# Delta rule of the prompt in a two-layer hybrid decoder step: both chunks' scores and triangular inverses side by side

## The chip, the cores and the metric

The kernel runs on one core of one Trainium2 chip. The metric is device time in microseconds (us), the median of several executions. The kernel is one inference step of a two-layer decoder, 256 prompt tokens and 64 sample tokens (8 sequences of 8), with all weights read once from memory.

## The reference, cut to what matters

Each layer projects the 320 tokens with one big matrix, runs three mixers side by side (a gated delta rule, differential attention on a paged cache, gated linear attention), projects back, and runs a gated feed-forward network. What the change touches is the gated delta rule of the prompt. It works in chunks of tokens; inside a chunk it solves a unit lower triangular system for each head:

```python
kk = jnp.einsum('bihd,bjhd->bhij', ki, ki)
A = jnp.where(strict, kk * dmat * bh[..., :, None], 0.0)
M = jnp.eye(C, dtype=jnp.float32) + A
sol = lax.linalg.triangular_solve(M, jnp.concatenate([vbeta, kbd], -1), left_side=True, lower=True, unit_diagonal=True)
u = sol[..., :DV] - jnp.einsum('bhck,bhkv->bhcv', sol[..., DV:], S)
o = (q * exp(gh)) @ S + qk @ u ;  S_new = S * exp(glast) + kw^T @ u
```

There are 6 heads of 128 x 128. The kernel uses chunks of 128 tokens for the prompt, so two chunks (c = 0, 1), and treats the heads in two halves of three (hs = 0, 1). The scores and the inverse of M do not depend on the running state S; only what follows them does.

## The kernel before, in words

**The dense stream.** Weights come in units of 128 x 512 numbers (`raw`), are split into a high part (`whi`, ACT) and a low part (`wlo`, DVE), and multiplied on PE with the activations (`xh`, `xl`, and `oA`, `oB`, `act..` in the later projections), three matmuls of 128x320 for each 128 x 128 block. There are 19392 such dense matmuls in a program; their order is fixed. They are recorded by `emit_unit` (L1035); the rest of the work (the mixers, normalisation) is written as tasks (generators) that are stepped between units and record their operations too. The output projection's first unit needs `oA`, the gated result of the delta rule, and everything else that it reads (L1062 `drain`).

**What sets the order.** All operations are first recorded with their dependences, then `order` (L536) makes a list schedule: for each engine it takes the available operation with the longest tail. On PE it has three classes, dense matmuls, small matmuls that fill the array, and small matmuls on 32- or 64-row tiles ("part"), and it holds part work back until enough of it has gathered or one has waited long:

```python
sticky, PB, PW = False, 1000.0, 3000.0                      # L578
elif part and (0 not in cl or sum(ops[i].cost for i in part) >= PB or t - min(ops[i].est for i in part) >= PW):  # L610
    want = 2
```

Once issued, the order on each engine is that of the program: an instruction whose inputs are late holds up all that stand behind it on its engine. All instructions carry the line of the helper that issues them, L696 (DMA issues of the cache pages: L2031), so in the profile they are told apart by their tiles. `g` (in programs `g_0_90`, `g_1_...`) is the private memory of the delta rule of the prompt, `gen` and `geng` are the two general memories, `c` and `blkC` belong to the linear attention, `bank` is PSUM.

**The delta rule tasks.** `gdn_prompt(l, hs)` (L1647) treats one half: for each chunk it makes the decayed scores (`decay_scores`, L1602; `AQ` holds query and key scores), the inverses of the 32 x 32 diagonal blocks by five levels of masked products (`inverse`, L1553), assembles the 128 x 128 inverse in a block `U` of its own, and then applies it to values and state. The two halves use the same 2700 words (L1652), so the second starts when the first has ended; inside a half, chunk 1 started when chunk 0 had ended.

`gdn_sample(l, hs)` (L1795) is the same for the 64 sample tokens. It treats its three heads one after the other in one buffer: a head's state is loaded (`in_sgdn`, 512 KB, L1816), multiplied with keys and queries, updated, and stored (`out_gs`, L1863); only then can the next head's state be loaded. The second half (hs = 1) takes its 1920 and 704 words from the general memory `mem` (L1799), where the attention task holds 3640 words (L1920) until its last values are done (`attn_values`, L2121, released at L1947). The gated linear attention (`gla_main`, L2172) starts behind a flag that this sample task sets when it has its memory (L1802). When prompt and sample halves have ended, `gdn_main` (L1440) multiplies with the gate (`gate`, L1533) and writes `oA`, which the output projection waits for.

Of the kernel before, what the change touches and what calls it, by code (L numbers as in the profile page):

```python
# [18 lines left out]
ALU = mybir.AluOpType  # L19
# [724 lines left out]
def emit(nc, pool, psp, T, O, coff, ioff, n_pages):  # L744
# [63 lines left out]
    def cs(name, rows=slice(0, 128)):  # L808
        a, n = coff[name]
        return cst[rows, a:a + n]  # L810
# [91 lines left out]
    def ap(h):  # L902
        return h[1][2]
# [649 lines left out]
    def inverse(aq, k, R, get, keep):  # L1553

        nb = R // 32
        lv = (1, 2, 4, 8, 16) if R == 128 else (1, 2, 4)
        nl = len(lv)
        Ad = yield from get(32 * k)
        ad = ap(Ad)[0:R].rearrange("p (h i) -> p h i", h=k)
        for b in range(nb):  # L1560
            sl = slice(32 * b, 32 * b + 32)
            (G.tensor_copy if b % 2 else V.tensor_copy)(ad[sl], aq[sl, :, 1, sl])
        LT = yield from get(nl * 32 * k)
        lt = ap(LT)[0:R].rearrange("p (s h i) -> p s h i", s=nl, h=k)
        msk = cs("ms", slice(0, R)).rearrange("p (s i) -> p s i", s=5)[:, 0:nl]
        for s in range(nl):
            tt(V, lt[:, s], ad, msk[:, s:s + 1, :].to_broadcast([R, k, 32]), ALU.mult)
        fr(Ad)
        yield
        TU = yield from keep(64 * k)  # L1570
        tu = ap(TU)[0:R].rearrange("p (t h i) -> p t h i", t=2, h=k)
        idb = cs("idb", slice(0, R))[:, None, :].to_broadcast([R, k, 32])
        tf, tf_ = (ap(TU)[0:R, 32 * k * t:32 * k * t + 32 * k] for t in range(2))
        tt(V, tu[:, 1], idb, lt[:, 0], ALU.subtract)
        V.transpose(tf, tf_)
        yield
        Ph = yield from get(32 * k)
        p_ = ap(Ph)[0:R].rearrange("p (h i) -> p h i", h=k)
        for s in range(1, nl):
            bb = yield from bank()  # L1580
            pv_ = banks[bb][0:R, 0:32 * k].rearrange("p (h i) -> p h i", h=k)
            for h in range(k):
                for b in range(nb):
                    sl = slice(32 * b, 32 * b + 32)
                    mm(pv_[sl, h], lt[sl, s, h], tu[sl, 0, h])
            A.copy(p_, pv_)
            fb(bb)
            yield
            bb = yield from bank()
            pw = banks[bb][0:R, 0:32 * k].rearrange("p (h i) -> p h i", h=k)  # L1590
            for h in range(k):
                for b in range(nb):
                    sl = slice(32 * b, 32 * b + 32)
                    mm(pw[sl, h], tu[sl, 1, h], p_[sl, h])
            tt(V, tu[:, 0], tu[:, 0], pw, ALU.subtract)
            fb(bb)
            V.transpose(tf_, tf)
            yield
        fr(LT, Ph)
        return TU  # L1600

    def decay_scores(l, g, h0, k, get, keep):  # L1602

        X = L
        col = X["col"]
        c0, n = CC[g]
        R = n
        bb = yield from bank()
        b = banks[bb][0:R, 0:k * n].rearrange("p (h i) -> p h i", h=k)
        mng = cs("mneg") if g < 2 else cs("mneg8", slice(0, 64))  # L1610
        for h in range(k):
            tr(b[:, h], col["gc"][0:R, g, h0 + h:h0 + h + 1].to_broadcast([R, R]), slice(0, R))
        Dh = yield from get(k * n)
        d = ap(Dh)[0:R].rearrange("p (h i) -> p h i", h=k)
        for h in range(k):
            stt(d[:, h], b[:, h], col["gc"][0:R, g, h0 + h:h0 + h + 1], mng, ALU.subtract, ALU.add)
        fb(bb)
        A.activation(d, d, AF.Exp)
        yield
        AQ = yield from keep(k * 2 * n)  # L1620
        aq = ap(AQ)[0:R].rearrange("p (h t i) -> p h t i", h=k, t=2)
        for h in range(k):
            bb = yield from bank()
            b = banks[bb][0:R, 0:2 * n].rearrange("p (t i) -> p t i", t=2)
            for t, nm in enumerate(("q", "k")):
                mm(b[:, t], X["k"][:, h0 + h, c0:c0 + n], X[nm][:, h0 + h, c0:c0 + n])
            stt(aq[:, h], b, col["s"][0:R, g, h0 + h:h0 + h + 1], d[:, h:h + 1, :].to_broadcast([R, 2, n]), ALU.mult, ALU.mult)
            fb(bb)
            if h == 1:
                yield  # L1630
        yield
        fr(Dh)
        return AQ, aq

    def rms_factor(m, out, t1, c=None):

# [10 lines left out]
    def gdn_prompt(l, hs):  # L1647
# [3 lines left out]
        h0 = 3 * hs  # L1651
        R, M = yield from private(2700, lambda: (mem4[0],))  # L1652
        get = lambda n: get_from(n, lambda: (M,))
        for c in range(2):
            cc = slice(c * 128, c * 128 + 128)
            AQ, aq = yield from decay_scores(l, c, h0, 3, get, get)
            TU = yield from inverse(aq, 3, 128, get, get)
            tu = ap(TU).rearrange("p (t h i) -> p t h i", t=2, h=3)
            U = yield from get(384)
            u = ap(U).rearrange("p (h i) -> p h i", h=3)  # L1660
            G.memset(ap(U), 0.0)
            for b in range(4):
                sl = slice(32 * b, 32 * b + 32)
                (G.tensor_copy if b % 2 else A.copy)(u[sl, :, sl], tu[sl, 1])
            bb = yield from bank()
            pv_ = banks[bb][:, 0:96].rearrange("p (h i) -> p h i", h=3)
            for h in range(3):
                for a in range(2):
                    up, lo = slice(64 * a, 64 * a + 32), slice(64 * a + 32, 64 * a + 64)
                    mm(pv_[lo, h], aq[up, h, 1, lo], tu[up, 0, h])  # L1670
            Ph = yield from get(96)
            p_ = ap(Ph).rearrange("p (h i) -> p h i", h=3)
            for a in range(2):
                lo = slice(64 * a + 32, 64 * a + 64)
                A.copy(p_[lo], pv_[lo])
            fb(bb)
            T64 = yield from get(192)
            t64 = ap(T64).rearrange("p (h i) -> p h i", h=3)
            G.memset(ap(T64)[0:64], 0.0)
            V.tensor_copy(t64[0:32, :, 0:32], tu[0:32, 0])  # L1680
            V.tensor_copy(t64[32:64, :, 32:64], tu[32:64, 0])
            yield
            bb = yield from bank()
            pv_ = banks[bb][:, 0:96].rearrange("p (h i) -> p h i", h=3)
            for h in range(3):
                for a in range(2):
                    up, lo = slice(64 * a, 64 * a + 32), slice(64 * a + 32, 64 * a + 64)
                    mm(pv_[up, h], p_[lo, h], tu[lo, 1, h])
                mm(pv_[32:64, h], tu[32:64, 1, h], p_[32:64, h])
            for a in range(2):  # L1690
                up, lo = slice(64 * a, 64 * a + 32), slice(64 * a + 32, 64 * a + 64)
                tsc(V, u[up, :, lo], pv_[up], -1.0, ALU.mult)
            A.mul(t64[32:64, :, 0:32], pv_[32:64], -1.0)
            fb(bb)
            fr(TU, Ph)
            yield
            bb = yield from bank()
            pv_ = banks[bb][:, 0:192].rearrange("p (h i) -> p h i", h=3)
            for h in range(3):
                mm(pv_[64:128, h], aq[0:64, h, 1, 64:128], t64[0:64, h])  # L1700
            P64 = yield from get(192)
            p64 = ap(P64).rearrange("p (h i) -> p h i", h=3)
            A.copy(p64[64:128], pv_[64:128])
            fb(bb)

            bb = yield from bank(2)
            for h in range(3):
# [8 lines left out]
                A.mul(kw[:, h], banks[bb[0]][:, h * 128:h * 128 + 128], col["es"][:, c, h0 + h:h0 + h + 1])  # L1716
                tsc(V, vs[:, h], banks[bb[1]][:, h * 128:h * 128 + 128], col["nk"][:, c, h0 + h:h0 + h + 1], ALU.mult)
            fb(*bb)
            yield
            bb = yield from bank()  # L1720
            pv_ = banks[bb][:, 0:192].rearrange("p (h i) -> p h i", h=3)
            for h in range(3):
                mm(pv_[0:64, h], p64[64:128, h], u[64:128, h, 64:128])
            tsc(V, u[0:64, :, 64:128], pv_[0:64], -1.0, ALU.mult)
            fb(bb)
            fr(P64, T64)

            if c == 1:
                bb = yield from bank()
# [7 lines left out]
            bb = yield from bank()  # L1737
            b = banks[bb][:, 0:384].rearrange("p (h v) -> p h v", h=3)
            for h in range(3):
                mm(b[:, h], u[:, h], vs[:, h])  # L1740
            WS = yield from get(384)
            ws = ap(WS).rearrange("p (h v) -> p h v", h=3)
            A.copy(ws, b)
            fb(bb)
            fr(U, VS)
            OH = yield from get(384)
            o = ap(OH).rearrange("p (h v) -> p h v", h=3)
            if c == 1:
# [7 lines left out]
            bb = yield from bank()  # L1756
            b = banks[bb][:, 0:384].rearrange("p (h v) -> p h v", h=3)
            for h in range(3):
                mm(b[:, h], aq[:, h, 0], ws[:, h])
            if c == 1:  # L1760
                tt(V, o, o, b, ALU.add)
            else:
                V.tensor_copy(o, b)
            fb(bb)
            fr(AQ)
            bb = yield from bank()
            b = banks[bb][:, 0:384].rearrange("p (h v) -> p h v", h=3)
            for h in range(3):
# [26 lines left out]
    def gdn_sample(l, hs):  # L1795
# [5 lines left out]
        get = lambda n: get_from(n, lambda: (M1,))  # L1801
        set_flag(("gsmem", l, hs))  # L1802
        tmp = lambda n: get_from(n, lambda: (M2,))
        AQ, aq = yield from decay_scores(l, 2, h0, 3, tmp, get)
        TU = yield from inverse(aq, 3, 64, tmp, get)

        osm = ap(AQ)[64:128].rearrange("p (h v) -> p h v", h=3)
# [826 lines left out]
```

## Time and profile before

| | us |
|---|---|
| median of 3 runs | 3294.72 |
| lowest and highest of them | 3292.67 and 3296.1 |
| the profiled execution's own time | 3294.52 |
| its span (first to last instruction) | 3292.7 |
| PE busy | 3235.2 (98%) |
| PE weight loads busy | 3072.3 (93%) |
| DVE, ACT, POOL busy | 1959.6, 1493.2, 359.7 (60%, 45%, 11%) |
| mean granted TensorE clock | 0.994 of full speed |

PE busy is the union of modelled matmul durations; a matmul's duration (0.31 us for a dense one) is longer than the distance to the next one, so the pace of the dense stream is read by counting matmuls in a stretch. The delta rule of a layer lies in the first part of the layer (about 60 to 560 us in layer 0, 1700 to 2193 us in layer 1), between dense matmuls of the input projection.

### The profile page before, as it was taken

The page shows a single profiled execution, that of the slowest core. Times are in us where ns is not written, and L with a number is a line of the kernel's source. Part 1 is how long each engine was busy: PE and PEld are TensorE (multiplying, and loading weights), DVE is VectorE, ACT ScalarE, POOL GpSimd, SP SyncE. Part 2 cuts the span into 40 slices and gives each one's busy share as a digit, 9 for nine tenths or more (in the row PEclk, how much of TensorE's full clock was granted, in tenths as well). Part 3 has the DMA queues.
Part 4 walks back from the last instruction along what each step waited for, and adds up shares of the span by engine and source line. Part 5 has one row for each costly group of instructions (what it writes and reads, how often), then busy time and mean ns, then how long its engine had stood idle before and what let it go on. Part 6 is the DMA issues. An engine that isn't in the chain of part 4 may idle for free.

```text
span 3292.7 us, 67703 instructions
## 1 busy us (share of the span) xinstructions
PE 3235.2 (98%) x25466; PEld 3072.3 (93%) x25466; DVE 1959.6 (60%) x3780; ACT 1493.2 (45%) x3069; POOL 359.7 (11%) x604
## 2 busy tenths in 40 slices
PE   9999999999999999999999999989999999999997
PEld 9987887899999999999999887878999999999997
DVE  5676558885444445544776764588854544454446
ACT  5454444465433443344574444444744334433444
POOL 0233323200000000000002333231000000000000
PEclk9999999999999999999999999999999999999998
DMA  7466764455555555555555667534555555555553
GB/s 228 142 194 212 220 194 129 137 148 157 151 149 150 151 151 148 151 150 151 150 154 154 193 217 231 170 127 138 147 151 151 151 149 150 151 150 149 150 151 115
DMA packets 264393, 527.70 MB, mean 160 GB/s; under 512 B 31362, under 2 KB 33026, under 8 KB 263938
## 3 DMA queue, kind: packets, MB, share of 16 engines
q1 hardware_dynamic: 243586, 456.26, 48.4%
q0 software_dynamic: 20480, 67.13, 6.3%
q8 instruction: 199, 3.26, 0.4%
q14 instruction: 128, 1.05, 0.1%
HBM read 506.25 MB, written 16.36 MB: 159 GB/s over the span
## 4 chain that ended last, share of the span: by engine, by line
PE 76%; issue 2%; DVE 1%; DMA 1%; ACT 0%; POOL 0%; POOLq 0%; SPq 0%; ACTq 0%; DVEq 0%
PE bank L696 76%; DVE gen L696 0%; POOLq L2029 0%; DMA geng<-in_ck 0%; DVE wlo L696 0%; DVE geng L696 0%; POOL geng L2031 0%; DVE blkB L696 0%; DMA out_gs<-gen 0%; DMA gen<-in_sgdn 0%; DMA c<-in_sgdn 0%; ACT blkB L696 0%; DVE c L696 0%; POOL blkB L696 0%; ACT accq L696 0%
## 5 line engine op out<-in xcount | busy, mean ns | idle before, releaser
L696 DVE TENSOR_TENSOR wlo<-raw,whi 128x512 fp32r<-128x512 f32 x1616 | 1124.2, 696 | 1091.4 <-PE bank L696 893.5
L696 ACT CAST whi<-raw 128x512 fp32r<-128x512 f32 x1616 | 1001.7, 620 | 1403.6 <-PE bank L696 1340.0
L696 PE MATMUL bank<-xh,wlo 128*128 128x320 f32 (+1 forms) x4544 | 1418.6, 312 | 0.0
L696 PE MATMUL bank<-xh,whi 128*128 128x320 f32 (+1 forms) x4544 | 1413.3, 311 | 4.7 <-ACT xh L696 4.7
L696 PE MATMUL bank<-xl,whi 128*128 128x320 f32 (+1 forms) x4544 | 1414.6, 311 | 0.1
L696 PEld LDWEIGHTS bank<-xh,whi 128*128 128x128 f32 x4544 | 856.1, 188 | 12.8 <-issue 5.7
L696 PEld LDWEIGHTS bank<-xh,wlo 128*128 128x128 f32 x4544 | 857.8, 189 | 7.6 <-issue 3.9
L696 PEld LDWEIGHTS bank<-xl,whi 128*128 128x128 f32 x4544 | 855.4, 188 | 7.6 <-issue 4.4
L696 PE MATMUL bank<-actA,whi 128*128 128x320 f32 x1152 | 255.5, 309 | 0.0
L696 PEld LDWEIGHTS bank<-actA,whi 128*128 128x128 f32 x1152 | 192.9, 188 | 0.4
L696 PE MATMUL bank<-actA,wlo 128*128 128x320 f32 x576 | 178.1, 309 | 0.0
L696 PE MATMUL bank<-actB,whi 128*128 128x320 f32 x768 | 170.5, 309 | 0.0
L696 PE MATMUL bank<-actCh,whi 128*128 128x320 f32 x448 | 138.3, 309 | 0.0
L696 PE MATMUL bank<-actCl,whi 128*128 128x320 f32 x448 | 138.3, 309 | 0.0
L696 PE MATMUL bank<-actCh,wlo 128*128 128x320 f32 x448 | 138.3, 309 | 0.0
L696 PEld LDWEIGHTS bank<-actB,whi 128*128 128x128 f32 x768 | 128.6, 188 | 0.0
L696 PE MATMUL bank<-actB,wlo 128*128 128x320 f32 x384 | 118.6, 309 | 0.0
L696 PE MATMUL bank<-geng,gen 128*32 128x256 f32 (+5 forms) x968 | 101.8, 466 | 7.3 <-DMA geng<-in_ck 4.4
L696 PEld LDWEIGHTS bank<-actA,wlo 128*128 128x128 f32 x576 | 108.2, 188 | 0.1
L696 POOL COPY gen<-g 128x24 f32<-128x24 f32 x18 | 5.9, 328 | 878.1 <-DMA g<-in_scv 871.2
L2031 POOL DMA_DIRECT2D geng<-in_ck x128 | 70.7, 552 | 274.3 <-DVE actA L696 137.8
L696 PE MATMUL bank<-oA,whi 128*128 128x320 f32 x384 | 92.7, 325 | 5.3 <-ACT oA L696 4.8
(291 smaller groups left out, 3324.1 us busy)
## 6 DMA issues: line engine op xcount, KB each, us to landing
raw<-in_wgu SPq DMA_DIRECT2D x704, 256.0 KB
raw<-in_win SPq DMA_DIRECT2D x434, 256.0 KB
raw<-in_wd SPq DMA_DIRECT2D x352, 256.0 KB
geng<-in_ck POOLq DMA_DIRECT2D x128, 256.0 KB, 3.8
geng<-in_cvp POOLq DMA_DIRECT2D x128, 256.0 KB, 3.7
raw<-in_wout SPq DMA_DIRECT2D x128, 256.0 KB
c<-in_sgdn SPq DMA_DIRECT2D x6, 512.0 KB
out_gs<-c SPq DMA_DIRECT2D x6, 512.0 KB
```

What stands on the lines that cost most here:

```text
L696: fn(*[real(x) for x in a], **{k: real(v) for k, v in kw.items()})
L2031: G.eng.dma_start(out[:, k * 512:k * 512 + 512], src[l, ds(reg, 1)].rearrange(pat))
```

## The change

`inverse` no longer makes all masked copies of the diagonal blocks at once (`LT` of five parts) but one level at a time, in one buffer that is rewritten after each level's product. `gdn_prompt` makes the scores of both chunks first, into one `AQ` of 1536 words, then one inverse for six (chunk, head) pairs, and assembles it in place over the key scores (`u = aq[:, :, 1, :]`) instead of in a cleared block `U`. What follows (values, state, output) stays one chunk after the other, with the last product of the assembly moved ahead of it. `decay_scores` writes where its caller says. The sample task calls the same `inverse` and `decay_scores`.

```diff
@@ inverse
-        LT = yield from get(nl * 32 * k)
-        for s in range(nl):
-            tt(V, lt[:, s], ad, msk[:, s:s + 1, :].to_broadcast([R, k, 32]), ALU.mult)
-        fr(Ad)
+        LT = yield from get(32 * k)
+        def level(s):
+            tt(V, lt, ad, msk[:, s:s + 1, :].to_broadcast([R, k, 32]), ALU.mult)
+        level(0)
...
+        level(1)
...
-                    mm(pv_[sl, h], lt[sl, s, h], tu[sl, 0, h])
+                    mm(pv_[sl, h], lt[sl, h], tu[sl, 0, h])
             A.copy(p_, pv_)
             fb(bb)
+            if s + 1 < nl:
+                level(s + 1)
@@ gdn_prompt
+        AQ = yield from get(1536)
+        aq = ap(AQ).rearrange("p (h t i) -> p h t i", h=6, t=2)
+        u = aq[:, :, 1, :]
+        for c in range(2):
+            yield from decay_scores(l, c, h0, 3, get, aq[:, 3 * c:3 * c + 3])
+        TU = yield from inverse(aq, 6, 128, get, get)
...
+                mm(pv_[lo, h], u[up, h, lo], tu[up, 0, h])
...
         for c in range(2):
             cc = slice(c * 128, c * 128 + 128)
-            AQ, aq = yield from decay_scores(l, c, h0, 3, get, get)
-            TU = yield from inverse(aq, 3, 128, get, get)
...
-            U = yield from get(384)
-            G.memset(ap(U), 0.0)
...
-                mm(b[:, h], u[:, h], vs[:, h])
+                mm(b[:, h], u[:, 3 * c + h], vs[:, h])
...
-            fr(AQ)
+            M.release((AQ[1][0] + 768 * c, 768, None))
```

The list schedule is made anew, so the change moves instructions on every engine. Three places on PE, in layer 0.

First, a level of the inverse (`g` is the private memory of the prompt's delta rule), between dense matmuls of the input projection. Before:

```order
L696 MATMUL bank_80<-xl,whi 128x320
L696 MATMUL bank_80<-xh,wlo 128x320
L696 MATMUL bank_86<-cst,gen 128x128 x2
L696 MATMUL bank_85<-g_0_90 32x32 x12
L696 MATMUL bank_80<-xh,whi 128x320
```

Now:

```order
L696 MATMUL bank_81<-xl,whi 128x320
L696 MATMUL bank_81<-xh,wlo 128x320
L696 MATMUL bank_83<-g_0_90 32x32 x24
L696 MATMUL bank_81<-xh,whi 128x320
L696 MATMUL bank_81<-xl,whi 128x320
```

Two groups of 12 products on 32 x 32 tiles have become one of 24.

Second, the sample task's last head: the product of its state with keys and queries (`bank<-gen,sq` and `bank<-gen,sk`), with what stands ahead of it. Before:

```order
L696 MATMUL bank_80<-xl,whi 128x320
L696 MATMUL bank_80<-xh,wlo 128x320
L696 MATMUL bank_80<-xh,whi 128x320
L696 MATMUL bank_84<-gen,sq_625 32x512
L696 MATMUL bank_84<-gen,sk_91 32x512
L696 MATMUL bank_84<-gen,sq_625 32x512
L696 MATMUL bank_84<-gen,sk_91 32x512
L696 MATMUL bank_83<-geng 32x32 x12
L696 MATMUL bank_82<-geng 32x32 x4
```

Now:

```order
L696 MATMUL bank_85<-cst,sk_91 64x128
L696 MATMUL bank_85<-cst,sv 64x128
L696 MATMUL bank_81<-xh,wlo 128x320
L696 MATMUL bank_82<-gen,sq_625 32x512
L696 MATMUL bank_82<-gen,sk_91 32x512
L696 MATMUL bank_82<-gen,sq_625 32x512
L696 MATMUL bank_82<-gen,sk_91 32x512
L696 MATMUL bank_83<-geng 32x32 x12
L696 MATMUL bank_86<-geng 32x32 x4
```

The dense matmul just ahead of it is number 2509 of the program before; now it is number 2592, the last one of the input projection.

Third, what stands directly ahead of the output projection's first matmul on `oA`. Before:

```order
L696 MATMUL bank_81<-xh,whi 128x320
L696 MATMUL bank_81<-xl,whi 128x320
L696 MATMUL bank_81<-xh,wlo 128x320
L696 MATMUL bank_83<-cst,gen 64x128 x3
L696 MATMUL bank_79<-oA_6182,whi 128x320 x2
```

Now:

```order
L696 MATMUL bank_84<-gen 32x128 x2
L696 MATMUL bank_86<-geng 32x32 x4
L696 MATMUL bank_85<-geng 32x32 x4
L696 MATMUL bank_82<-geng 32x32 x4
L696 MATMUL bank_83<-gen 64x128
L696 MATMUL bank_82<-gen 128x512
L696 MATMUL bank_85<-gen 128x512
L696 MATMUL bank_84<-geng 32x32 x6
L696 MATMUL bank_86<-geng 32x32 x6
L696 MATMUL bank_83<-geng 32x32 x6
L696 MATMUL bank_84<-cst,gen 128x64 x3
L696 MATMUL bank_86<-geng 32x32 x6
```

Behind the last row follows the same first matmul on `oA`. The sample task's steps for its last head (`gen`) and some of the linear attention (`geng`) stand there where dense matmuls of the input projection stood before.

## Rows read from the trace of the kernel before

**Rows 1.** Section 1 of the page: busy time, share, instructions of each engine.

```profile
PE 3235.2 (98%) x25466; PEld 3072.3 (93%) x25466; DVE 1959.6 (60%) x3780; ACT 1493.2 (45%) x3069; POOL 359.7 (11%) x604
```

**Rows 2.** Busy time by stretch: stretch and length, engines' busy time (x instructions), clock.

```profile
1200.00:1500.00 300.00, 300.00 (x2048) 299.84 (x2048) 144.95 (x234) 117.31 (x199) 0.00 (x0) 1.00 0.55 150
```

**Rows 3.** PE's timeline (start, duration) round one group of the inverse.

```profile
276.88 0.31 PE L696 MATMUL bank<-xl,whi 128*128 128x320 f32 x1
277.12 0.39 PE L696 MATMUL bank<-g 32*32 32x32 f32 x24
277.44 0.41 PE L696 MATMUL bank<-xh,wlo 128*128 128x320 f32 x1
```

**Rows 4.** All PE products on `g`: durations min/median/max in ns, starts, forms.

```profile
L696 PE MATMUL bank<-g x2016: 188/191/276, 127.2 to 2091.2; 32*32 32x32 f32 x162, 128*128 128x128 f32 x13, 64*64 64x64 f32 x9
```

**Rows 5.** PE's timeline: two attention steps, and the second sample half's first product.

```profile
443.86 1.06 PE L696 MATMUL bank<-geng,gen 128*32 128x512 f32 x8
...
450.70 1.06 PE L696 MATMUL bank<-geng,gen 128*32 128x512 f32 x8
...
471.97 0.33 PE L696 MATMUL bank<-sq,sk 128*64 128x64 f32 x2
```

**Rows 6.** Timeline of PE and SP: the first head's state load of that half.

```profile
493.01 0.25 PE L696 MATMUL bank<-gen 32*32 32x32 f32 x4
...
493.36 0.33 SPq L696 DMA_DIRECT2D gen<-in_sgdn  x1
...
497.60 0.59 PE L696 MATMUL bank<-gen,sq 128*32 128x512 f32 x1
```

**Rows 7.** Timeline of PE and SP: from the second head's update to the third's product.

```profile
527.97 1.13 PE L696 MATMUL bank<-gen 32*128 32x512 f32 x4
...
534.96 0.33 SPq L696 DMA_DIRECT2D gen<-in_sgdn  x1
...
538.64 0.59 PE L696 MATMUL bank<-gen,sq 128*32 128x512 f32 x1 [1.51 <-DMA gen<-in_sgdn]
```

**Rows 8.** Timeline of all engines: from the third head's product to `oA`.

```profile
541.69 0.97 DVE L696 SCALAR_TENSOR_TENSOR gen<-gen 64x128 f32<-64x128 f32 x1
...
544.85 0.41 PE L696 MATMUL bank<-gen 32*32 32x128 f32 x4
...
546.63 0.38 PE L696 MATMUL bank<-geng 64*32 64x32 f32 x12 [1.37 <-DVE geng L696]
...
548.45 0.43 PE L696 MATMUL bank<-gen 64*64 64x128 f32 x2
...
555.73 0.37 PE L696 MATMUL bank<-cst,gen 64*128 64x64 f32 x3 [1.24 <-DVE gen L696]
...
558.26 2.85 POOL L696 TENSOR_TENSOR blkB<-blkB,sv 128x320 f32<-128x320 f32 x1 [3.09 <-ACT whi L696]
...
561.23 0.86 POOL L696 TENSOR_TENSOR blkB<-blkB,sv 128x320 f32<-128x320 f32 x1
...
562.63 0.41 PE L696 MATMUL bank<-oA,whi 128*128 128x320 f32 x1 [2.48 <-ACT oA L696]
```

**Rows 9.** Dense matmuls on `whi` (two of three) in that stretch, by stretch.

```profile
538.60:562.60 24.00, 12.95 (x55) 1.00 0.33 101
```

**Rows 10.** Dense matmuls on `wlo` (one of three) in that stretch.

```profile
538.60:562.60 24.00, 8.66 (x28) 1.00 0.33 101
```

**Rows 11.** PE's timeline, layer 1: the same two ends.

```profile
2169.39 0.59 PE L696 MATMUL bank<-gen,sq 128*32 128x512 f32 x1 [1.84 <-DMA gen<-in_sgdn]
...
2193.25 0.41 PE L696 MATMUL bank<-oA,whi 128*128 128x320 f32 x1 [2.31 <-ACT oA L696]
```

**Rows 12.** PE's timeline behind the first products on `oA`: a linear attention step.

```profile
579.83 0.75 PE L696 MATMUL bank<-cst,blkC 128*128 128x128 f32 x3 [1.67 <-DVE gen L696]
```

**Rows 13.** Busy time by stretch: a stretch of 3.4 us at a low granted clock.

```profile
580.00:583.40 3.40, 3.40 (x16) 3.40 (x16) 1.24 (x3) 0.28 (x3) 0.00 (x0) 0.50 0.22 82
```

More of the change, by code (lines that the diff above doesn't have):

```diff
@@ L1562, in inverse @@
             (G.tensor_copy if b % 2 else V.tensor_copy)(ad[sl], aq[sl, :, 1, sl])
-        LT = yield from get(nl * 32 * k)
-        lt = ap(LT)[0:R].rearrange("p (s h i) -> p s h i", s=nl, h=k)
-        msk = cs("ms", slice(0, R)).rearrange("p (s i) -> p s i", s=5)[:, 0:nl]
-        for s in range(nl):
-            tt(V, lt[:, s], ad, msk[:, s:s + 1, :].to_broadcast([R, k, 32]), ALU.mult)
-        fr(Ad)
+        LT = yield from get(32 * k)
+        lt = ap(LT)[0:R].rearrange("p (h i) -> p h i", h=k)
+        msk = cs("ms", slice(0, R)).rearrange("p (s i) -> p s i", s=5)
+        def level(s):
+            tt(V, lt, ad, msk[:, s:s + 1, :].to_broadcast([R, k, 32]), ALU.mult)
+        level(0)
         yield
@@ L1573, in inverse @@
         tf, tf_ = (ap(TU)[0:R, 32 * k * t:32 * k * t + 32 * k] for t in range(2))
-        tt(V, tu[:, 1], idb, lt[:, 0], ALU.subtract)
+        tt(V, tu[:, 1], idb, lt, ALU.subtract)
         V.transpose(tf, tf_)
+        level(1)
         yield
@@ L1598, in inverse, with decay_scores @@
             yield
-        fr(LT, Ph)
+        fr(Ad, LT, Ph)
         return TU
-    def decay_scores(l, g, h0, k, get, keep):
+    def decay_scores(l, g, h0, k, get, aq):
         X = L
@@ L1619, in decay_scores @@
         yield
-        AQ = yield from keep(k * 2 * n)
-        aq = ap(AQ)[0:R].rearrange("p (h t i) -> p h t i", h=k, t=2)
         for h in range(k):
@@ L1632, in decay_scores @@
         fr(Dh)
-        return AQ, aq
     def rms_factor(m, out, t1, c=None):
@@ L1653, in gdn_prompt @@
         get = lambda n: get_from(n, lambda: (M,))
+        AQ = yield from get(1536)
[4 more added lines that the diff above has]
+        TU = yield from inverse(aq, 6, 128, get, get)
+        tu = ap(TU).rearrange("p (t h i) -> p t h i", t=2, h=6)
+        bb = yield from bank()
+        pv_ = banks[bb][:, 0:192].rearrange("p (h i) -> p h i", h=6)
@@ new lines, in gdn_prompt @@
+        for h in range(6):
+            for a in range(2):
+                up, lo = slice(64 * a, 64 * a + 32), slice(64 * a + 32, 64 * a + 64)
+                mm(pv_[lo, h], u[up, h, lo], tu[up, 0, h])
+        Ph = yield from get(192)
+        p_ = ap(Ph).rearrange("p (h i) -> p h i", h=6)
+        for a in range(2):
+            lo = slice(64 * a + 32, 64 * a + 64)
+            A.copy(p_[lo], pv_[lo])
+        fb(bb)
+        for b in range(4):
+            sl = slice(32 * b, 32 * b + 32)
+            (G.tensor_copy if b % 2 else A.copy)(u[sl, :, sl], tu[sl, 1])
@@ new lines, in gdn_prompt @@
+        T64 = yield from get(384)
+        t64 = ap(T64).rearrange("p (h i) -> p h i", h=6)
+        G.memset(ap(T64)[0:64], 0.0)
+        V.tensor_copy(t64[0:32, :, 0:32], tu[0:32, 0])
+        V.tensor_copy(t64[32:64, :, 32:64], tu[32:64, 0])
+        yield
+        bb = yield from bank()
+        pv_ = banks[bb][:, 0:192].rearrange("p (h i) -> p h i", h=6)
+        for h in range(6):
+            for a in range(2):
+                up, lo = slice(64 * a, 64 * a + 32), slice(64 * a + 32, 64 * a + 64)
+                mm(pv_[up, h], p_[lo, h], tu[lo, 1, h])
+            mm(pv_[32:64, h], tu[32:64, 1, h], p_[32:64, h])
@@ new lines, in gdn_prompt @@
+        for a in range(2):
+            up, lo = slice(64 * a, 64 * a + 32), slice(64 * a + 32, 64 * a + 64)
+            tsc(V, u[up, :, lo], pv_[up], -1.0, ALU.mult)
+        A.mul(t64[32:64, :, 0:32], pv_[32:64], -1.0)
+        fb(bb)
+        fr(TU, Ph)
+        yield
+        bb = yield from bank()
+        pv_ = banks[bb][:, 0:384].rearrange("p (h i) -> p h i", h=6)
+        for h in range(6):
+            mm(pv_[64:128, h], u[0:64, h, 64:128], t64[0:64, h])
+        P64 = yield from get(384)
@@ L1654, in gdn_prompt @@
+        p64 = ap(P64).rearrange("p (h i) -> p h i", h=6)
+        A.copy(p64[64:128], pv_[64:128])
+        fb(bb)
+        yield
+        bb = yield from bank()
+        pv_ = banks[bb][:, 0:384].rearrange("p (h i) -> p h i", h=6)
+        for h in range(6):
+            mm(pv_[0:64, h], p64[64:128, h], u[64:128, h, 64:128])
+        tsc(V, u[0:64, :, 64:128], pv_[0:64], -1.0, ALU.mult)
+        fb(bb)
+        fr(P64, T64)
         for c in range(2):
             cc = slice(c * 128, c * 128 + 128)
-            AQ, aq = yield from decay_scores(l, c, h0, 3, get, get)
@@ L1657, in gdn_prompt @@
-            TU = yield from inverse(aq, 3, 128, get, get)
-            tu = ap(TU).rearrange("p (t h i) -> p t h i", t=2, h=3)
-            U = yield from get(384)
-            u = ap(U).rearrange("p (h i) -> p h i", h=3)
-            G.memset(ap(U), 0.0)
[L1662 to L1704, printed above, removed]
             bb = yield from bank(2)
@@ L1718, in gdn_prompt @@
             fb(*bb)
[L1719 to L1726, printed above, removed]
             if c == 1:
@@ L1744, in gdn_prompt @@
             fb(bb)
-            fr(U, VS)
+            fr(VS)
             OH = yield from get(384)
@@ L1758, in gdn_prompt @@
             for h in range(3):
-                mm(b[:, h], aq[:, h, 0], ws[:, h])
+                mm(b[:, h], aq[:, 3 * c + h, 0], ws[:, h])
             if c == 1:
@@ L1803, in gdn_sample @@
         tmp = lambda n: get_from(n, lambda: (M2,))
-        AQ, aq = yield from decay_scores(l, 2, h0, 3, tmp, get)
+        AQ = yield from get(384)
+        aq = ap(AQ)[0:64].rearrange("p (h t i) -> p h t i", h=3, t=2)
+        yield from decay_scores(l, 2, h0, 3, tmp, aq)
         TU = yield from inverse(aq, 3, 64, tmp, get)
```

## The prediction

> **What bounds the kernel now.** I read the page's busy shares first, then the stretches of the dense stream, then the timeline where PE stands still. PE is busy 98% of the span, DVE 60%, ACT 45%, POOL 11% [rows 1], so what the change takes from DVE, ACT and POOL is worth nothing by itself; only work and waits on PE count. The dense stream alone goes at 300 us / 2048 = 0.1465 us a matmul [rows 2], and 19392 of them make 2841 us of the profiled execution's 3294.5 us. The remaining 450 us are small products and waits. Two things in them can move: what a separate group of small products costs PE, and the place where the output projection waits for `oA`. The second is a wait now, although the busy share hides it: from the third head's product at 538.64 to the first matmul on `oA` at 562.63 it takes 24.0 us [rows 8, 7], in which only 55 + 28 = 83 dense matmuls run [rows 9, 10], 12.2 us at the dense pace; PE stands idle for 1.4, 1.2 and 2.5 us there, and 1.5 us just ahead of it for the state's load. Layer 1 repeats it: 23.9 us, waits of 1.8 and 2.3 us [rows 11]. So the sample half's chain is already late at the end of the input projection.
>
> **Part by part: fewer groups.** The number of products on PE is the same; what falls is the number of times that PE turns from the dense stream to a group of small ones. One group of 12 products (24 passes) of the inverse lies between two dense matmuls that start 0.56 us apart instead of 0.1465, so it costs 0.41 us [rows 3]. Its passes start over 0.39 less the 0.19 of one pass [rows 4], that is 0.20 us; the other 0.21 us are paid for the turn and saved where two groups become one. At most 48 pairs can merge (12 steps of the inverse and its assembly, two halves, two layers), 10 us. But many of them stand beside other small work already. Counted in the two programs' order, unbroken stretches of tiled products fall from 200 to 172, and stretches of full-array small products rise from 205 to 217: 16 fewer, 3.4 us at 0.21 us. I take -3.4 us, bounds -10 and 0. The masks level by level put a 128x192 multiplication between two products of the chain; DVE is not what PE waits for in this part, and the chain of the prompt ends long before anything needs it, so I cost it at nothing. Its cover is the dense stream of the input projection: the prompt's delta rule now ends some 300 dense matmuls earlier in the program's order (1886 instead of 2190 ahead of it).
>
> **Part by part: what comes later for it.** That early end is no gain, because the sample task's second half does not wait for the prompt but for the attention's memory (the 1920 words at L1799), and the attention ends later. Its eight value steps of the second group ran with prompt work between them; the scheduler holds tiled work back until enough has gathered, and a lone attention step now waits out the 3000 of L578. In the order they stand 30 dense matmuls apart before, 56 now. Before, a step took 450.70 - 443.86 = 6.84 us [rows 5]; now 26 x 0.1465 = 3.8 us more. The second sample half, which began at 471.97 behind dense matmul 2224 [rows 5], begins behind 2358. Its chain keeps its length and runs out of dense matmuls to lie under. Four places in each layer:
>
> 1. From the second head's update to the third head's product, 527.97 to 538.64: 10.7 us, ended by the wait for the state's load [rows 7]. The store, the load and their order on SP stay (one weight load stands between them before and now), so the length stays. 42 dense matmuls stood in it, 22 stand now: 20 x 0.1465 = +2.9 us of idle PE. The same in both bounds.
>
> 2. From that product to `oA`, 24.0 us with 83 dense matmuls; now none. 12.2 us of cover go, and the segment shortens by what was waiting for the dense stream. The key sum ended at 541.69 + 0.97 = 542.66, its product came at 544.85 [rows 8]: 2.0 us can go. The next product, at 548.45, stands behind a linear-attention group at 546.63 + 0.38 [rows 8]: 1.4 us can go, and the 1.4 us of that group's own wait perhaps. From there the chain is bare (PE idles until 555.73 and again until 562.63), save that the gate's product on POOL took 2.85 us where the next of its shape took 0.86 [rows 8]: perhaps 2.0 more. Bounds: nothing goes (24.0) or all (17.3). I take 20, nearer the rows that surely go. Cost 20 - (24.0 - 12.2) = +8.2 us, bounds +5.5 and +12.2.
>
> 3. The front: from the last inverse product to the first head's product 493.01 to 497.60, load issued at 493.36 [rows 6], with 20 dense matmuls between before and 15 now (+0.7), and no dense matmul any more where 17 stood ahead of that inverse product (2.5 if all of it is wait). I take +1.0, bounds 0 and +2.5.
>
> 4. Behind `oA` the linear attention follows at closer distance: 25 dense matmuls ahead of its next group instead of 35, 23 fewer in all until its sample part ends, 1.5 and 3.4 us of cover; it already waits there (1.7 us at 579.83 [rows 12]). I take +1.0, bounds 0 and +3.4.
>
> **The clock.** After such waits the granted clock stands at 0.50 for 3.4 us [rows 13], which is the 1.2 GHz level; if all of that lies under the dense stream it loses half of it, 1.7 us. The new wait is long enough to add one of these in a layer, but most of it would fall into the wait itself: +0.5, bounds 0 and +1.7 us. The Trainium skill (TensorE: Matmul & The Clock Gate, Part 1) puts it so: "the default state is throttled, and activity releases the throttle"; rows 13, right after a wait, agree, and by that rule alone a thinner stretch would cost more than my term, which is rival three.
>
> **The sum.** Per layer 2.9 + 8.2 + 1.0 + 1.0 + 0.5 = 13.6 us, two layers 27.2, less 3.4: +23.8 us on the profiled execution's 3294.5, that is 3318 us. That execution lies 0.2 us under the median of the runs, so nothing is to be corrected. Bounds: (2.9 + 5.5) x 2 - 10 = +7 and (2.9 + 12.2 + 2.5 + 3.4 + 1.7) x 2 = +45.
>
> **The rivals.**
>
> *One: the chain shrinks to its bare length and all groups merge.* Then +7 us, 3302 us. For it: PE's small work was behind the dense stream at two of the chain's steps. Against: PE idles at its other three, where nothing dense can be blamed. Chance 0.14.
>
> *Two: faster.* The stretch ahead of `oA` is paced by the dense stream throughout, through the weights' conversion on DVE and ACT that its steps queue behind and the weight loads ahead of the state's load on SP; with no dense matmul there it contracts by all 15 us that a layer loses in cover, and 10 us of merged groups are left: 3285 us. It decides at 5 us a layer: if the two segments (34.7 us before) fall to under 24.5 us, the change wins. Against: waits for the load, for DVE and for ACT `oA` ended last in both layers [rows 7, 8, 11]. Chance 0.06.
>
> *Three: the clock falls with the wait.* Two more stretches at half clock under dense work in each layer (2 x 1.7), and small products on the chain at half speed (their durations sum to 3.3 us, taken as 3 a layer [rows 7, 8]): 2 x 6.4 = 13 us more, 3331 us. For it: PE would have some 20 us of little work. Chance 0.12.
>
> My forecast keeps 0.68.
>
> **How the numbers follow.** The likeliest case gives 3318 us, with 3305 to 3331 of its own. The range takes in most of rivals one and three: 3302 to 3333 us. About 0.2% (6.6 us) is what a measurement of this kernel tells from no change, so slower begins at 3301.3 and faster ends at 3288.1. Slower: the forecast, rival three and a third of rival one, 0.86 with the forecast's lower tail taken off a little. Same: the rest of rival one and parts of two, 0.08. Faster: 0.06.
>
> **What would show it.** In the changed kernel's timeline: the third head's product directly behind the input projection's last dense matmul, and between it and the first `oA` some 20 us with no dense matmul, in both layers, PE waiting there for DVE, ACT and the state's load; about 40 us earlier in each layer, attention steps some 9 to 10 us apart instead of 6.8; groups of 48 passes on `g` costing about 0.6 us where two cost 0.82. The granted clock low in that stretch. I am wrong if the stretch is under 15 us, if the sample's second half starts no later than before relative to the dense stream, or if the first 400 us of a layer gain more than 5 us.

## The result and the profile after

The changed kernel takes 3326.16 us (median of 4 runs, 3324.96 to 3330.07) against 3295.41 us (3292.67 to 3296.62) for the kernel before on the same chip: ratio 1.010, 95% interval 1.0085 to 1.0115. It is slower by 31 us; 3318 us was forecast. Its profiled execution took 3327.04 us, its span is 3325.4 us.

The page, section 1, shows almost the same busy time of PE as [rows 1] (3235.2 us before):

```profile
PE 3236.4 (97%) x25466; PEld 3078.3 (93%) x25466; DVE 1959.2 (59%) x3692; ACT 1488.6 (45%) x3029; POOL 344.5 (10%) x576
```

Span less busy time is 57.5 us before and 89.0 us now: the loss is time in which PE stands still. What PE waits for, in the changed kernel (releaser, sum in us, times, longest):

```profile
PE bank L696 <- DVE gen L696: 11.8, 9, 2.0
PE bank L696 <- DMA gen<-in_sgdn: 10.5, 3, 5.2
PE bank L696 <- DVE geng L696: 10.1, 13, 2.2
PE bank L696 <- ACT oA L696: 8.8, 2, 4.8
...
PE bank L696 <- DVE blkB L696: 3.7, 2, 2.0
PE bank L696 <- DMA c<-in_sgdn: 2.9, 2, 1.6
```

The same view of the kernel before, the same releasers (`blkB` is not among its rows):

```profile
PE bank L696 <- DVE gen L696: 8.4, 8, 1.7
PE bank L696 <- ACT oA L696: 4.8, 2, 2.5
...
PE bank L696 <- DVE geng L696: 4.3, 6, 1.5
PE bank L696 <- DMA gen<-in_sgdn: 3.4, 2, 1.8
...
PE bank L696 <- DMA c<-in_sgdn: 0.7, 3, 0.3
```

The new waits are those of the sample task's last head: its state's load, DVE on `gen`, the linear attention beside it (`geng`), `oA`. PE's timeline shows the place in layer 0 (answers to [rows 7] and [rows 8]):

```profile
545.67 1.13 PE L696 MATMUL bank<-gen 32*128 32x512 f32 x4
...
555.68 1.03 PE L696 MATMUL bank<-gen,sq 128*32 128x512 f32 x1 [3.75 <-DMA gen<-in_sgdn]
...
563.75 2.08 PE L696 MATMUL bank<-gen 32*128 32x512 f32 x4 [2.16 <-DVE geng L696]
...
568.82 0.55 PE L696 MATMUL bank<-cst,gen 64*128 64x64 f32 x3 [1.82 <-DVE gen L696]
...
574.66 0.64 PE L696 MATMUL bank<-oA,whi 128*128 128x320 f32 x1 [4.83 <-ACT oA L696]
```

and in layer 1 (answers to [rows 11]):

```profile
2192.48 1.13 PE L696 MATMUL bank<-gen 32*128 32x512 f32 x4
...
2203.98 1.03 PE L696 MATMUL bank<-gen,sq 128*32 128x512 f32 x1 [5.23 <-DMA gen<-in_sgdn]
...
2221.72 0.63 PE L696 MATMUL bank<-oA,whi 128*128 128x320 f32 x1 [3.96 <-ACT oA L696]
```

From the third head's product to `oA` lie 18.98 and 17.74 us. By stretch (stretch and length, PE's busy time (x count), clock, DMA share, GB/s), with dense matmuls on `whi` alone, there is none in it, where [rows 9] had 55:

```profile
545.60:555.60 10.00, 3.24 (x15) 0.91 0.63 188
555.60:574.60 19.00, 0.00 (x0) 0.50 0.11 41
574.60:581.40 6.80, 5.27 (x14) 0.52 0.01 2
581.40:584.80 3.40, 1.25 (x5) 1.00 0.37 95
```

The granted clock is 0.50, the 1.2 GHz level, through the whole bare stretch (the one without dense matmuls) and, by the mean of 0.52, until some 0.3 us before the end of the 6.8 us of dense work behind it.

**Where the 31 us are.** The time from one dense matmul's start to the next, from PE's records, less 0.1465 us [rows 2], is what the rest of the program costs PE. I split it three ways, from the first dense matmul to the last: PE idle in stretches with small work between two dense matmuls; the rest of these stretches (the small work itself and its turns); and what dense matmuls with nothing between them lose (above all to the clock). Before: 344 stretches, 347.0 us of small work, 30.2 us idle, 46.4 us lost by the dense stream. The table gives the differences to that, in us, with the median of each kernel's runs; the stretches in it count one less than those in the expectations, which count the program's ends too. They are read from one profiled execution of each kernel, which can lie some us from its median (e11_after_attn 4 us under it, e10_before_pb1500 4 us over it); and every edit remakes the whole order, so a difference of a few us has no single cause here.

| kernel | median | stretches | small work | PE idle | dense stream | sum |
|---|---|---|---|---|---|---|
| changed kernel | 3326.16 | 340 | -3.3 | +29.4 | +6.2 | +32.3 |
| e4_before_late | 3328.32 | 331 | +2.6 | +30.1 | -1.4 | +31.4 |
| e10_before_pb1500 | 3330.36 | 339 | +7.8 | +32.9 | -0.6 | +40.0 |
| e11_after_attn | 3302.22 | 346 | -3.6 | +5.9 | +0.8 | +3.1 |
| e2_after_mem | 3279.70 | 322 | -8.4 | -3.8 | -4.5 | -16.6 |
| e3_before_mem | 3297.90 | 336 | +1.5 | -0.7 | +1.1 | +1.9 |
| e8_mem_pb1500 | 3272.38 | 318 | -10.7 | -6.3 | -5.0 | -22.0 |
| e1_pw | 3317.62 | 374 | +6.5 | +12.7 | +3.8 | +22.9 |
| e7_mem_pw500 | 3325.35 | 380 | +8.5 | +16.0 | +3.1 | +27.6 |
| e5_before_levels | 3302.46 | 364 | +1.8 | +2.8 | +1.2 | +5.9 |
| e9_fill | 3324.67 | 339 | +13.8 | +18.2 | -0.7 | +31.3 |

### The profile page after: what moved, and what is told of

Its sections match the earlier page's. It is cut to its first block, busy times and chain, and to the rows that moved or that the text cites. A ratio compares the mean times of both kernels' runs of the same rounds, so it can differ in the third digit from the quotient of the medians.

```text
span 3325.4 us, 67533 instructions
## 1 busy us (share of the span) xinstructions
PE 3236.4 (97%) x25466; PEld 3078.3 (93%) x25466; DVE 1959.2 (59%) x3692; ACT 1488.6 (45%) x3029; POOL 344.5 (10%) x576
## 4 chain that ended last, share of the span: by engine, by line
PE 77%; DVE 2%; issue 1%; DMA 1%; POOL 0%; ACT 0%; POOLq 0%; ACTq 0%; DVEq 0%; SPq 0%
PE bank L696 77%; DVE gen L696 1%; DVE geng L696 1%; DVE blkB L696 0%; DMA geng<-in_ck 0%; DMA gen<-in_sgdn 0%; POOLq L2035 0%; DMA c<-in_sgdn 0%; DMA out_gs<-gen 0%; DVE wlo L696 0%; POOL geng L696 0%; DMA gen<-in_wa 0%; POOL geng L2037 0%; ACT blkB L696 0%; DVE oA L696 0%
## 5 line engine op out<-in xcount | busy, mean ns | idle before, releaser
L696 PEld LDWEIGHTS bank<-xh,wlo 128*128 128x128 f32 x4544 | 859.4, 189 | 16.5 <-issue 13.1
```

The source lines that it names most:

```text
L696: fn(*[real(x) for x in a], **{k: real(v) for k, v in kw.items()})
```

## The experiments

The theory: the sample task's second half comes late, because the attention, whose lone value steps are held back, keeps the memory that this half needs; its chain then stands bare ahead of `oA`. Rival A: the new inverse costs the time itself. Rival B: the clock does, without the lateness.

**The lateness alone, in the kernel before (e4).** `hold` is an earliest time on the list schedule's own clock, in ns.

```diff
@@ decay_scores, kernel before
+        if g == 2 and h0:
+            prog.hold = (438.7e3, 1944.0e3)[l]
         for h in range(k):
             tr(b[:, h], ...)
+        prog.hold = 0.0
```

> The kernel before, with one number more: the first transposes of the sample task's second half get an earliest time, so that this half stands where it stands in the changed kernel (its three heads' products behind dense matmuls 2421, 2510 and 2591 of each layer, against 2426, 2509 and 2590 there, 2312, 2402 and 2487 in the kernel before). Nothing of the new inverse is in it. Theory (the loss comes from the late second sample half, which runs out of dense matmuls to lie under): the changed kernel's segments cost 9.5 us a layer there and 3.7 us behind oA, so some 26 us in all, 3321 us, at least 3313; a stretch of 17 to 20 us without dense matmuls ahead of oA in both layers. Rival A (the inverse for six pairs and the masks level by level cost it): within 5 us of the kernel before, 3290 to 3300. Rival B (the clock alone, lowered by what the new inverse does to PE): as rival A, and no low granted clock ahead of oA.

Measured: 3328.32 us, ratio 1.0099 (1.0082 to 1.0116), 7 us above what I expected, PE idle +30.1 us. None of the new inverse is in it, and it loses what the changed kernel loses. Its timeline in layer 0:

```profile
554.38 1.03 PE L696 MATMUL bank<-gen,sq 128*32 128x512 f32 x1 [4.78 <-DMA gen<-in_sgdn]
...
562.45 2.08 PE L696 MATMUL bank<-gen 32*128 32x512 f32 x4 [2.16 <-DVE geng L696]
...
575.50 1.30 PE L696 MATMUL bank<-oA,whi 128*128 128x320 f32 x2 [4.95 <-ACT oA L696]
```

and the first 18.40 of the 21.1 us from that product to `oA`, all engines:

```profile
554.40:572.80 18.40, 8.84 (x165) 4.02 (x165) 14.11 (x31) 8.35 (x19) 8.25 (x6) 0.50 0.08 31
```

The waits are near those of the changed kernel (3.75, 2.16 and 4.83 us), and the clock is 0.50 here too. Rival A would have left this kernel where it was. It falls as the main cause, and so does B as a thing of its own: the low clock comes with the lateness, and the dense stream loses no more here than in the kernel before (-1.4 us). What the low clock adds to the products of the bare stretch itself, no run here separates.

**The link to the attention, undone in the changed kernel (e11).**

```diff
@@ order, changed kernel
 elif part and (0 not in cl or sum(...) >= PB or t - min(...) >= PW
+               or any(ops[i].lab == "attn_values" for i in part)):
```

> The changed kernel with one link of the chain undone: the list schedule no longer holds the attention's value steps back until enough tiled work has gathered. They then stand 34 dense matmuls apart (56 in the changed kernel, 30 in the kernel before), the attention's last stands behind 2169 (2330; 2196), the sample task's second half begins behind 2196 (2357; 2236 before) and ends behind 2523 (2591; 2567). Its memory is that of the changed kernel, and the inverse too. Theory (the lone value steps that wait hold up the memory, and so that half): PE's waits fall back to those of the kernel before and the merged groups' 3 us stay, less 7 stretches of small work more (2 us): 3286 to 3299. If the lateness came from something else in the change: still over 3315.

Measured: 3302.22 us, ratio 1.0016 (1.0006 to 1.0025); that is 4.7 us above the kernel before measured beside it (3297.51 us). The inverse, its memory and the sample task are those of the changed kernel; the value steps alone are let in at once. Some 26 of the 31 us are gone, PE's idle time falls from +29.4 to +5.9 us, and the dense stream's loss from +6.2 to +0.8. So the lateness came through the attention. It ended 3 us above the top of what I expected; the rest is in the main idle time that the undone link does not touch, above all ahead of the attention's first scores. The waits view of this kernel (one line number higher, as the edit adds a line) has no row for ACT's `oA` any more, 8.8 us in the changed kernel, and the wait for the state's load is 5.5 us instead of 10.5:

```profile
PE bank L697 <- DVE gen L697: 11.4, 6, 2.4
PE bank L697 <- DMA gen<-in_sgdn: 5.5, 4, 1.8
...
PE bank L697 <- DVE blkB L697: 3.9, 2, 2.0
...
PE bank L697 <- DMA c<-in_sgdn: 3.1, 4, 1.3
```

In the changed kernel the `blkB` wait is this row, and layer 1 has its like:

```profile
194.17 0.49 PE L696 MATMUL bank<-blkB 64*128 64x128 f32 x2 [2.01 <-DVE blkB L696]
```

**The memory link, undone (e2), and its control (e3).**

```diff
@@ gdn_sample, changed kernel (e2); the same in the kernel before (e3)
-        R2, M2 = yield from private(1920, lambda: (mem if hs else X["memC"][0],))
-        R1, M1 = yield from private(704, lambda: (mem if hs else X["memC"][1],))
+        if hs:
+            yield from until(("gp", l, 1))
+        R2, M2 = yield from private(1920, lambda: (mem4[0] if hs else X["memC"][0],))
+        R1, M1 = yield from private(704, lambda: (mem4[0] if hs else X["memC"][1],))
```

> The changed kernel, but the sample task's second half takes its 1920 and 704 words from the memory that the prompt's delta rule leaves, as soon as its second half has ended, and waits no longer for the attention's. Its last products then stand behind dense matmul 2253 of a layer instead of 2591, the attention's last value step behind 2157 instead of 2330. Theory: the chain lies under the input projection again, so the 13 us a layer at the tail and behind oA go, and so does the waiting ahead of it: 3285 to 3300 us, below the kernel before by what the merged groups save (2 us a layer measured in small work, 3291 us). Rival A: the new inverse keeps its price, 3315 us or more. Rival B (the clock falls because of the new inverse's groups): 3305 to 3315, low granted clock where the inverse runs.

> The kernel before with the same other memory for the sample task's second half as in e2_after_mem: the control for it. There the prompt's delta rule ends late (2214), so the sample's last products stand behind dense matmul 2556 instead of 2567. Theory: same as the kernel before within 4 us, 3291 to 3299, as nearly nothing moves at the tail; and e2_after_mem lies below it by the saving of the merged groups, 1 to 7 us. Rival A: e2_after_mem lies some 25 us above it.

Measured: e2 3279.70 us, ratio 0.9943 (0.9930 to 0.9957), better than both kernels and below what I expected; e3 3297.90 us, 1.0004 (0.9994 to 1.0013), no change. The same inverse that lost 31 us wins 17 us when the sample half may start as soon as the prompt's memory is free. The product that stood at 555.68 behind a 3.75 us wait stands here without one:

```profile
479.95 0.62 PE L696 MATMUL bank<-g,sq 128*32 128x512 f32 x1
```

e2 lies 18.5 us under e3 by the table's sums: 9.9 us of small work, 3.1 us of PE's idle time, 5.6 us of the dense stream. The products on `g` (each record's distance to the next, less idle time) take 58.1 us instead of 64.6, so about a third is the merged groups. That the rest is work near the end of the input projection that was crowded in the kernel before and is not any more is my reading; no run shows it by itself. The early end of the prompt is worth something once somebody can use its memory.

**The holding time (e1, e7).**

```diff
@@ order: changed kernel (e1), e2_after_mem (e7)
-        sticky, PB, PW = False, 1000.0, 3000.0
+        sticky, PB, PW = False, 1000.0, 500.0
```

> The changed kernel with one number changed: small tiled products on PE are held back for at most 500 instead of 3000 in the list schedule. The lone attention value steps then stand 37 dense matmuls apart instead of 56, the attention's last stands behind 2049 instead of 2330, the sample's last product behind 2315 instead of 2591. Theory: the chain is covered again and the loss of 31 us goes, less what more and smaller groups of tiled products cost (0.21 us a turn): 3290 to 3305 us. Rival A: 3320 or more.

> e2_after_mem with the holding time of e1_pw (500 instead of 3000). The sample's last products stand behind dense matmul 2026, so no part of the tail can be bare; the small work lies in 381 stretches between dense matmuls instead of 323 in e2_after_mem. It tells why e1_pw (375 stretches, 3317.6 us) stayed 38 us above e2_after_mem. If what is left there is the tail: 3279 to 3285. If it is the turns at my price of 0.21 us: 58 x 0.21 = 12 us above e2_after_mem, 3292. If a turn costs what e1_pw suggests (38 us for 52 more, 0.7 us with the waits that smaller groups bring): 3315 to 3325.

Measured: e1 3317.62 us (1.0059, 1.0046 to 1.0073), e7 3325.35 us (1.0095, 1.0080 to 1.0111), at the top of its highest guess. I was wrong on e1: covering the tail by holding less costs most of what it gives. e7 says why: with no bare tail at all it is 46 us slower than e2. Its 58 more stretches of small work cost 16.9 us themselves (8.5 + 8.4), 0.29 us each on average, against the 0.21 us that I had taken; and PE idles 19.8 us more. Small groups let in early wait for their inputs: the two waits below are 7.7 us in 6 times and 3.8 us in 2 in e2. The waits view of e7:

```profile
PE bank L696 <- DMA geng<-in_ck: 10.7, 20, 1.3
PE bank L696 <- DVE blkB L696: 8.2, 2, 4.1
```

**The gathering threshold (e8, e10).**

```diff
@@ order: e2_after_mem (e8), kernel before (e10)
-        sticky, PB, PW = False, 1000.0, 3000.0
+        sticky, PB, PW = False, 1500.0, 3000.0
```

> e2_after_mem with the other threshold of the list schedule: tiled work is gathered to 1500 instead of 1000 before it is let in. 319 stretches instead of 323, the sample's last products behind dense matmul 2363 instead of 2253, still 228 dense matmuls ahead of the output projection. Lateness theory: it has slack enough, so the same as e2_after_mem within 5 us, 3275 to 3285. If what counts is how early the sample half ends, and not whether it is covered: some us slower than e2_after_mem.

> The kernel before with the threshold of e8_mem_pb1500 (1500 instead of 1000) and nothing else. There it gained 7 us; here the lone value steps of the attention come later, the sample task's second half begins behind dense matmul 2392 of a layer (2236 before, 2357 in the changed kernel), and its third head's product stands behind the last matmul of the input projection. Nothing of the new inverse and no other memory is in it, and the stretches of small work fall from 345 to 340. Theory (lateness): bare tail as in e4_before_late with some 35 dense matmuls less of cover, 3325 to 3340. If the lateness of that half does not matter by itself: 3290 to 3298, by the fewer stretches.

Measured: e8 3272.38 us, ratio 0.9934 (0.9920 to 0.9947), the fastest kernel here and 3 us under what I expected; e10 3330.36 us, 1.0107 (1.0090 to 1.0124). The same number loses 36 us where the chain has no slack, and gains 7 us by the medians where it has some (5 us by the table's sums; the intervals of the two ratios overlap, so the size of this gain is not sure). In e10 nothing of the change is present, and it loses in the same place: PE idle +32.9 us, waits for `oA` of 9.8 us against 4.8.

**The masks alone (e5).** The kernel before with the new `inverse` alone (the hunks of `inverse` in the diff above).

> The kernel before with one part of the change alone: the inverse makes its masked copies level by level in one buffer; the chunks stay one after the other. The sample's last products stand behind dense matmul 2543 of a layer (2567 before), so the tail is covered as before. Theory (lateness): within 6 us of the kernel before, 3290 to 3303; the small work now lies in 365 separate stretches between dense matmuls instead of 345, which at 0.21 us each would be +4 us. Rival A (the masks level by level cost it): 3310 or more, with PE waiting for DVE g.

Measured: 3302.46 us, ratio 1.0019 (1.0010 to 1.0028), 6 us, at the upper end of what I expected, with PE idle +2.8 us and no more. It has 20 stretches more, 5.8 us at 0.29 us; the records put only 1.8 us of it on small work, so the split of these 6 us stays open. Rival A's 20 us are not there.

**The clock (e9).**

```diff
@@ gdn_sample, changed kernel, last head of the second half
+        def fill(i, n):
+            for _ in range(n):
+                mm(banks[i][:, 192:512], xh[:, 0, 0:128], xh[:, 1, 0:NT])
...
+            if last: fill(bb[0], 6)
...
+                if last: fill(bb[a], 5)
...
+        if hs: fill(bb, 8)
```

> The changed kernel with 24 additional products a layer that nobody reads (xh by xh, 320 columns, into free columns of a bank already read), put into PE's waits between the third head's product and oA: 6 after the key sum's product, 10 after the state's update, 8 at the end. Theory with the clock as a separate term (the low clock of the bare tail runs on into the dense stream behind oA, 25 matmuls in 7.3 us there): PE keeps its clock or gets it back sooner, and the dense stream behind oA loses up to 3.2 us a layer less; the fillers themselves delay the chain by 0 to 1.5 us a layer: 3320 to 3327. Without effect of the fillers on the clock: 3326 to 3330.

Measured: 3324.67 us, ratio 1.0089 (1.0074 to 1.0105), no different from the changed kernel. The stretches:

```profile
559.40:578.30 18.90, 16.05 (x188) 10.20 (x189) 14.38 (x30) 9.24 (x21) 8.30 (x8) 0.50 0.08 30
...
578.30:581.70 3.40, 3.11 (x14) 2.19 (x13) 3.40 (x7) 1.13 (x3) 1.13 (x3) 0.79 0.00 0
581.70:585.10 3.40, 3.01 (x17) 2.48 (x18) 3.07 (x9) 2.18 (x4) 0.24 (x1) 1.00 0.31 66
```

PE was busy 16.05 of 18.90 us and the clock stayed at 0.50 all the same. Behind `oA` it came back sooner in layer 0: a mean of 0.79 over the first 3.4 us means full speed after some 1.4 us, where it took some 6.5 us without the fillers. In layer 1, where `oA` starts at 2224.19, it hardly did, 4.2 us against 4.6:

```profile
2224.20:2228.40 4.20, 4.20 (x15) 4.10 (x16) 4.20 (x7) 1.58 (x5) 1.17 (x2) 0.50 0.00 0
```

The dense stream's loss fell from +6.2 to -0.7 us. But e4 and e10, as late and without fillers, stand at -1.4 and -0.6 us, so the +6.2 us are not a price that a bare tail must pay, and the clock's share of the changed kernel's loss stays open. The time did not follow: by the dense matmuls' starts, the stretch behind `oA` is 2.1 and 3.2 us shorter in the two layers, while 4.4 us more were lost ahead of it; why is not shown. Whether fillers alone could pay is open.

## Why the prediction was right, and where it was short

**The bare tail: right.** [rows 7] to [rows 10] gave 34.7 us of chain at these two places, of which the cover of 103 dense matmuls (15.1 us) was to go. Measured in layer 0: first segment 10.01 us against 10.67, with 20 dense matmuls less, +2.3 (forecast +2.9); second 18.98 us against 23.99 and 83 dense matmuls less, +7.2 (forecast +8.2, of 20 us). Together 9.4 in layer 0 and 9.5 in layer 1, where 11.1 was forecast. The second head's update from which layer 1 counts before is this row:

```profile
2158.43 1.13 PE L696 MATMUL bank<-gen 32*128 32x512 f32 x4
```

A part of what these segments cost is the clock's: at 0.50 the third head's update takes 2.08 us, at full clock the second's takes 1.13, and the product with keys and queries 1.03 us against 0.59 [rows 7]. How much, in all, is open.

**Why it comes late: right.** The attention's steps are 9.4 us apart now, 6.84 us before [rows 5]:

```profile
454.56 1.07 PE L696 MATMUL bank<-geng,gen 128*32 128x512 f32 x8
...
463.96 1.06 PE L696 MATMUL bank<-geng,gen 128*32 128x512 f32 x8
```

e11 and e2 cut this link at its two ends: with e2 the whole loss went, with e11 26 of the 31 us.

**Fewer groups: right in size.** -3.4 us forecast; the products on `g` (distance to the next record, less idle time) take 45.7 us instead of 49.2. That all small work differs by as little, -3.3 us, is a net in which products of the sample task at the low clock take more (`gen` 24.2 us instead of 21.3, `gen,sk` 11.2 instead of 8.5). A group of 48 passes:

```profile
358.38 0.30 PE L696 MATMUL bank<-xh,wlo 128*128 128x320 f32 x1
358.61 0.62 PE L696 MATMUL bank<-g 32*32 32x32 f32 x48
359.16 0.41 PE L696 MATMUL bank<-xh,whi 128*128 128x320 f32 x1
```

0.78 us between two dense starts, 0.63 us over the pace, against twice 0.41 [rows 3]: 0.19 us saved where a pair merges. The 16 groups fewer of the forecast are not stretches between dense matmuls; of these there are only 4 fewer.

**The front: mis-sized, and the larger miss.** I took +1.0 us a layer and set the masks and the rest at nothing; with the 1.7 us a layer that fewer groups were to save, that is -0.7 us. Up to the second head's update where 103 dense matmuls more stand ahead of it, layer 0 is 545.67 - 527.97 - 103 x 0.1465 = 2.6 us later, layer 1 by the same sum (2192.48 - 2158.43, less layer 0's 15.7 us and the 15.1 us) 3.3 us, with the groups' saving in it. Split as in the table, PE idles 4.2 and 5.2 us more up to there and the dense stream loses 2.1 us more in each layer. I had not looked at what the remade order does to others: the attention's first scores wait 2.0 and 1.7 us for DVE in the two layers, and behind that wait the clock is at 0.50 (from 195.4 to 198.8 us, and from 1840.6 to 1844.0 us), which costs the dense stream 1.5 us each time. e11 and e2 keep that wait.

**Behind `oA` and the clock: mis-sized.** I took 1.0 us for waits and 0.5 us for the clock in a layer; the dense matmuls' starts show +3.7 in both. Split as in the table, that is 2.1 and 1.7 us more of PE's idle time and 2.2 and 2.0 us more lost by the dense stream, less 0.6 us of small work in layer 0. I read [rows 13] as one stretch of 3.4 us of which most would fall into the wait. The clock fell at about 554 us, ahead of the third head's product, and stayed low for some 6.5 us behind `oA` in layer 0 and 4.6 us in layer 1. Of the 6.2 us that the dense stream lost in all, where I had 1.0, some 4 lie here and 3 behind the waits of the attention's first scores, with 1 gained elsewhere. The Trainium skill (TensorE: Matmul & The Clock Gate, Part 1) has it that activity releases the throttle; the rows behind `oA` agree, with a delay that my term had not; the stretch of e9 with PE busy for 16.05 of 18.90 us shows no release. Rival three, at 3331 us, was nearer for that part, and the chain's small products did run slower, as it says; the chain was shorter than I took it all the same.

In sum per layer: 9.4 + 2.6 + 3.7 = 15.7 us and 9.5 + 3.3 + 3.7 = 16.5 us, 32 us in all, where 23.8 were forecast. Over both layers the front cost 7 us more than forecast, the part behind `oA` 4 us more, and the bare tail 3 us less. The mechanism is shown; that 3318 us lies only 8 us under the measured time is in part luck, as these misses offset each other.

## What to carry to other kernels

When a change makes one task end early, ask what its neighbours were doing in its shadow: here the attention's steps rode along with the prompt's groups, and alone they were held back, which kept a memory that the critical chain needed. Before an improvement is dropped, look who could use what it frees: the same inverse went from 31 us slower to 17 us faster by taking the sample task's words from the freed block. A batching threshold has no good value of its own; here it was worth what the slack of the chain behind it allowed (-7 us by the medians in e8, +36 us in e10).

## What was not expected of the hardware

A stretch in which PE was busy 16.05 of 18.90 us, with the clock at 0.50 when it began, kept that clock to its end (e9). In the changed kernel the clock was 0.50 from about 554 to 581 us, and came back only some 6.5 us into the dense stream (4.6 us in layer 1). Two merged groups of the inverse cost 0.19 us less than two apart, but splitting the small work into 58 more stretches cost 0.29 us each on average and somewhat more than that again in waits.
